# Decoder layer on one core: low parts of 18 weight blocks made by a ScalarE copy and an adding transfer instead of a VectorE subtraction

## The chip, the cores and the metric

The kernel runs on one core of one Trainium2 chip. The metric is the device time of one execution, in microseconds (us), as the median of several runs. The engines are PE (TensorE), with PEld for its weight loads, DVE (VectorE), ACT (ScalarE), POOL (GpSimd) and SP (SyncE, which here only starts transfers).

## The reference, cut to what matters

One layer for 256 tokens of 1024 features: a half-step SwiGLU FFN, a mixing block (attention beside a gated unit), a second half-step SwiGLU FFN, a final norm; each part has a shift, a scale and a gate that come from c. The change lies in the second FFN:

```
mod = c_act @ w_ada[l] + b_ada[l]
(sh1, sc1, gt1, sh2, sc2, gt2, sh3, sc3, gt3) = jnp.split(mod, N_MOD, axis=-1)
...
y = modulate(rmsnorm(h, norm_ffn2[l]), sh3, sc3)
h = h + 0.5 * gt3[:, None, :] * swiglu(y, w_ffn2_gu[l], w_ffn2_down[l])
return rmsnorm(h, norm_final)

def swiglu(x, w_gu, w_down):
    g, u = jnp.split(x @ w_gu, 2, axis=-1)
    return (jax.nn.silu(g) * u) @ w_down
```

All data is float32. The result has to be as exact as float32 products give it.

## The kernel before

**Products in three parts.** PE multiplies in float32r, a shorter form of float32. So each float32 operand is split exactly into a high part (its float32r rounding) and a low part (what is left), and each product is done three times: high by high, low of the activations by high of the weights, high of the activations by low of the weights (`mm3`, L383, and `out_rows`, L397).

**Blocks of weights.** `add_weight` (L201) makes one block of 128 x 1024 numbers, 512 KB, ready: a place `raw` (8 of them, `RBUFS`), a place `wh` and a place `wl` (10 of each, `WBUFS`); SP starts the load from DRAM into `raw` (L208); ACT copies `raw` to `wh`, which rounds it (L209); DVE writes `wl = raw - wh` (L210). `raw` is free again after that, `wh` and `wl` after the block's last product. A block of the second FFN's gate and up weights is named `gu2`, block b (0 to 10, 256 hidden features each) and quarter kq (0 to 3, 256 of the 1024 input features); a block of its down weights `d2`, b, k (k is 0 or 1).

**Order of the work in FFN 2.** `gate_up(b)` (L438) runs over the four quarters and in each over both tiles t of 128 tokens; a step `k_part` (L389) is 6 matmuls. After the third step the activations of the block before are transposed (`turn`, L426: PE `pa`, ACT `ah`, DVE `al`), after each tile's last quarter ACT makes silu and DVE the product with u (`act_t`, L419: `sg`, `a`). Then `down(b-2)` (L458) runs 24 matmuls. So one round takes 72 matmuls and 4 transposes and uses 6 blocks of weights. Blocks 0 and 1 run in another order at the end of a handwritten list of steps (`MIX`, L57).

**Who decides when a block is made.** The program's text is the order of each engine. After each `mm3` or matmul of `out_rows`, `tick` (L328) compares a model of DVE's time, `vec.t`, with one of PE's, `ten.t`. As long as DVE's is less than 1 us ahead, it writes the next item: a block of weights, if fewer than 10 are in use, or an item of the list `fill`. In FFN 2 `fill` still holds the gate `gt3`: 8 blocks `ada8_k` of 512 KB use the same `raw` places, and for each of them DVE adds `ada * c` to a sum `acc` (L249); then the sum is split (`ada_split`, L264: ACT `acch`, DVE `accl`) and PE spreads it over the partitions with 4 matmuls `pada` (`ada_row`, L275). `vec.t` grows by each instruction that is issued through `vec`.

POOL computes a few small things there (`rstd_of`, L349) and is idle for the rest of FFN 2. It has started three transfers of 4 KB before (L246).

Of the kernel before, what the change touches and what calls it, by code (L numbers as in the profile page):

```python
# [8 lines left out]
F32 = mybir.dt.float32  # L9
F32R = mybir.dt.float32r  # L10
AF = mybir.ActivationFunctionType
ALU = mybir.AluOpType
# [63 lines left out]
class Paced:  # L76
    """An engine, and the time in us that the instructions written for it so far will take."""

# [28 lines left out]
def tile_decoder_layer(ctx: ExitStack, tc, i, out):  # L107
    """The schedule is the order of this text: each engine runs what is written for it in order."""
    nc = tc.nc
# [13 lines left out]
    def unit(name, shape, dtype=F32):  # L123
        """2 KB per partition, of a common pool."""
        return units[0].tile(shape, dtype, tag="u", name=name)
# [21 lines left out]

# [1 line left out]
    c_one = const.tile([1, D], F32, name="c_one")  # L149
# [42 lines left out]

# [1 line left out]
    # A weight block arrives in float32 and is split exactly, w = wh + wl; a block of w_ada is  # L194
    # multiplied by c and summed. tick() starts the next ones: as many as have a place, and no more
    # than the vector engine does within LEAD us of the products written so far.
    weights, fill = [], []
    ready, unused, live = {}, set(), set()
    keep, fill_at, auto = [0], [0.0], [False]

    def add_weight(key, srcs, shape, n=1024):  # L201
        def run():
            nm = "_".join(str(x) for x in key)
            raw = wp.tile([P, 1024], F32, tag="raw", name=f"raw_{nm}", bufs=RBUFS)
            wh = wp.tile([P, 1024], F32R, tag="wh", name=f"wh_{nm}")
            wl = wp.tile([P, 1024], F32R, tag="wl", name=f"wl_{nm}")
            for view, src in srcs(raw[:, :n]):
                nc.sync.dma_start(view, src)  # L208
            nc.scalar.activation(wh[:, :n], raw[:, :n], AF.Copy)  # L209
            vec.tensor_tensor(wl[:, :n], raw[:, :n], wh[:, :n].bitcast(F32), op=ALU.subtract)  # L210
            ready[key] = (shape(wh[:, :n]), shape(wl[:, :n]))
            unused.add(key)
            live.add(key)

        weights.append((key, run))
# [21 lines left out]
    def ada_item(comp, k):  # L237
        """A gate: 128 rows of its columns, times c, added to the sum. A shift or a scale: 128 of
        its columns, which lie on the partitions, times c, summed."""
        def run():  # L240
            raw = wp.tile([P, 1024], F32, tag="raw", bufs=RBUFS, name=f"ada{comp}_{k}")
            if comp in GATES:
                if k == 0:
                    adaacc[comp] = const.tile([P, D], F32, tag="acc", name=f"acc{comp}", bufs=1)
                    nc.gpsimd.memset(adaacc[comp], 0.0)
                    nc.gpsimd.dma_start(adaacc[comp][0:1, :], i["b_ada"][0:1, comp * D:(comp + 1) * D])  # L246
                acc = adaacc[comp]
                nc.sync.dma_start(raw, i["w_gate"][GATES.index(comp), tsl(k), :])
                vec.scalar_tensor_tensor(acc, raw, c_col[:, k:k + 1], acc, op0=ALU.mult, op1=ALU.add)  # L249
            else:  # L250
                nc.sync.dma_start(raw, i["w_shsc"][COMPS.index(comp), tsl(k), :])
                ada_sum(comp, k, raw)

        fill.append((("ada", comp, k), run))
# [20 lines left out]
    def ada_row(comp, mul):  # L275
        """A gate as a row on every partition."""
        def run():
            r = const.tile([P, D], F32, tag="adarow", name=f"ada_row{comp}", bufs=2)
            for n in range(2):
                ah, al = adahl[comp][n]  # L280
                p = pst(f"pada{comp}_{n}")
                ten.matmul(p, onesr, ah, start=True, stop=False)
                ten.matmul(p, onesr, al, start=False, stop=True)
                nc.scalar.activation(r[:, nsl(n)], p, AF.Copy, scale=mul)
            adarow[comp] = r
        fill.append((("adar", comp), run))
# [3 lines left out]
    def ada_col(comp, ks=slice(0, KT)):  # L290
        """A shift or a scale, its features on the partitions."""
        if comp not in adacol:
            adacol[comp] = sm.tile([P, KT], F32, tag="adacol", name=f"ada_col{comp}")
        r = adacol[comp][:, ks]
        if comp in b_sh:
            vec.tensor_tensor(r, adaacc[comp][:, ks], b_sh[comp][:, ks], op=ALU.add)
        elif ks.stop - ks.start == 1:
            vec.scalar_tensor_tensor(r, adaacc[comp][:, ks], b_sc[comp][:, ks], n_w[comp][:, ks],
                                     op0=ALU.add, op1=ALU.mult)
        else:  # L300
            vec.tensor_tensor(r, adaacc[comp][:, ks], b_sc[comp][:, ks], op=ALU.add)
            vec.tensor_tensor(r, r, n_w[comp][:, ks], op=ALU.mult)
# [10 lines left out]
    def upto(items, key):  # L313
        """Runs the items up to and including the one of this name."""
        while any(k == key for k, _ in items):
            items.pop(0)[1]()

    def done(key):
        """The block of this name was used for the last time: its place goes to a later one."""
        live.discard(key)  # L320
# [26 lines left out]

# [1 line left out]
    def rstd_of(parts, name):  # L349
        """(sum of the partial mean squares + eps) ** -0.5, per token."""  # L350
        v = sm.tile([P, 1], F32, tag="var", name=f"v_{name}")
# [8 lines left out]
    def mean_sq(x, n, name, junk=None):  # L360
        """sum(x^2) / n over 512 features; n is 512 or 1024."""
        ss = sm.tile([P, 1], F32, tag="ss", name=f"ss_{name}", bufs=6)
# [4 lines left out]

# [1 line left out]
    yh = const.tile([P, KT, S], F32R, name="yh")  # L369
# [19 lines left out]
    def k_part(ps, t, kq, key, first=None, last=None):  # L389
        """A quarter of the reduction over the model's features."""  # L390
        wh, wl = need(key + (kq,))
# [5 lines left out]
    def out_rows(po, t, lh, ll, w, first, last):  # L397
        """The products that add 128 rows to po[t]; lh and ll are the operands."""
        wh, wl = w
# [11 lines left out]

# [1 line left out]
    class Ffn:  # L413
# [51 lines left out]
    class Chain:  # L465
        """After the last product of a token tile: h += gt * po, the norm, and what comes of it."""

# [33 lines left out]

# [1 line left out]
    gu1, d1, w_in, w_out = i["gu1"], i["w_ffn1_down"][0], i["w_in"], i["w_out"][0]  # L503
# [59 lines left out]

    # ---- FFN 1, its first products in slices of the reduction as the modulation arrives: the
    # steps, and OPEN, their order ----
    f1 = Ffn("1")
# [3 lines left out]
    def once(key, *before):  # L570
        """Notes a step, and that these came before it."""
        assert key not in seen and all(x in seen for x in before), key
        seen.add(key)
# [22 lines left out]
    def open_t(j, e):  # L596
        """Two slices of the features of x, turned."""
        assert (0, j) in xn and (1, j) in xn
# [66 lines left out]
    def open_m(j, x, c, t):  # L665
        """Slice j of the products of a block."""
        wh, wl = splits[j, x]
# [25 lines left out]
    def open_p():  # L693
        """Keeps the clock of the tensor engine up until there are products."""
        if "idle" not in first:
            first["idle"] = pst("idle")
        ten.transpose(first["idle"][:, 0:P], ident, ident)
# [7 lines left out]
    for b in range(NFIRST, NB):  # L705
        f1.gate_up(b, [waiting.pop(0) for _ in range(min(4, len(waiting)))])
        waiting.append(b)
        for x in DOWNS.get(b, ()):
# [3 lines left out]
            f1.down(x)  # L712
# [1 line left out]

# [38 lines left out]

# [1 line left out]
    def half_row(name):  # L755
# [31 lines left out]
    def step_gv(t):  # L787
        """gelu and layer norm of the gating unit's v."""
        once(("gv", t))
# [25 lines left out]

    # q and k: rotary embedding, then heads on the partitions
    qkT = {}
# [41 lines left out]
    def step_ga(q):  # L859
        """Four heads, both chunks."""  # L860
        once(("ga", q), ("gn", 0), ("gn", 1))
# [22 lines left out]

    # scores and softmax, queries on the partitions
    probs, sums = {}, {}
# [162 lines left out]
def _lay_out(a):  # L1049
    import numpy as np  # L1050

    def gate_up(w):
        """[block, quarter, partition, (slice, gate or up, column)]"""
        return w.reshape(4, 2, P, 2, NB, 256).transpose(4, 0, 2, 1, 3, 5).reshape(NB, 4, P, 1024)
# [45 lines left out]
```

## Time and profile before

| What | us |
|---|---|
| Median of three runs | 511.62 |
| The three runs | 511.62, 513.96, 511.62 |
| Span of the profiled execution, first to last instruction | 509.2 |
| Fastest run less that span (what lies around it) | 2.4 |

| Engine | busy us | share of the span |
|---|---|---|
| PE | 496.5 | 98% |
| DVE | 375.1 | 74% |
| ACT | 264.1 | 52% |
| POOL | 24.3 | 5% |

The page lists no time of the profiled execution other than its span, so 2.4 us are taken as lying around it, and its own time as 511.6 us, which is the median. FFN 2 runs from about 312 us to 497 us of the span. All times in the rows are counted from the span's start. Line numbers are those of the kernel before; in the changed kernel the same lines come 4 to 8 lines later.

### The profile page before, as it was taken

How to read it: one execution, taken by the hardware profiler on the slowest of the kernel's cores; microseconds unless marked ns; L12 is line 12 of the kernel's file. 1: busy time of each engine (PE TensorE's matmuls, PEld its weight loads, DVE VectorE, ACT ScalarE, POOL GpSimd, SP SyncE). 2: the span in 40 equal slices, each digit the busy share in tenths (PEclk: the TensorE clock that was granted, in tenths of full speed). 3: DMA queues.
4: the chain of work that ended last, by engine and by line, in shares of the span. 5: the costliest groups of instructions: out<-in, count | busy, mean ns of one | idle time of the engine just before them, and what ended most of it. 6: DMA issues, size and time to landing. Idle time of an engine off the chain costs nothing.

```text
span 509.2 us, 6450 instructions
## 1 busy us (share of the span) xinstructions
PE 496.5 (98%) x2297; PEld 404.7 (79%) x2297; DVE 375.1 (74%) x512; ACT 264.1 (52%) x405; POOL 24.3 (5%) x38
## 2 busy tenths in 40 slices
PE   6999999999999999999999999999999999999994
PEld 4788888888888887887788988888888888888883
DVE  4999889998787557899888999879654545455244
ACT  4655576544544443776676447864544354444112
POOL 3100000000000200100003221000000000000000
PEclk9999999999999999999999999999999999999998
DMA  8999879999998966459776768699865555540002
GB/s 281 398 371 376 328 236 340 413 408 325 338 308 314 362 208 207 136 196 322 259 258 242 240 196 287 215 325 331 340 205 189 187 168 202 181 152 1 0 2 82
DMA packets 38018, 126.38 MB, mean 248 GB/s; under 512 B 4449, under 2 KB 4449, under 8 KB 37986
## 3 DMA queue, kind: packets, MB, share of 16 engines
q1 hardware_dynamic: 37602, 125.44, 70.4%
q10 hardware_dynamic: 288, 0.52, 0.3%
q8 instruction: 18, 0.29, 0.2%
q14 instruction: 14, 0.11, 0.1%
q0 software_dynamic: 96, 0.01, 0.0%
HBM read 124.91 MB, written 1.05 MB: 247 GB/s over the span
## 4 chain that ended last, share of the span: by engine, by line
PE 92%; DVE 2%; issue 2%; DMA 1%; ACT 1%; POOL 1%; SPq 0%; POOLq 0%; ACTq 0%
PE pg L85 39%; PE po L85 21%; PE f L85 8%; PE pw L85 4%; PE pp_gv L85 2%; PE pp_v L85 2%; PE pp_q L85 2%; PE pp_k L85 2%; PE pp_gu L85 2%; PE pa L85 2%; PE psc L85 2%; DMA h<-in_x_dram 1%; PE pv L85 1%; PE pada L85 1%; PE ppT L85 1%
## 5 line engine op out<-in xcount | busy, mean ns | idle before, releaser
L85 PE MATMUL pg<-wh_gu,yh 128*128 128x512 f32 x288 | 115.4, 401 | 0.0
L85 DVE TENSOR_TENSOR wl_gu<-raw_gu,wh_gu 128x1024 fp32r<-128x1024 f32 x72 | 86.8, 1222 | 38.1 <-ACT wh_gu L209 37.9
L85 PE MATMUL pg<-wl_gu,yh 128*128 128x512 f32 x288 | 113.7, 395 | 0.0
L85 PE MATMUL pg<-wh_gu,yl 128*128 128x512 f32 x288 | 113.6, 394 | 0.0
L209 ACT ACTIVATE wh_gu<-raw_gu 128x1024 fp32r<-128x1024 f32 x72 | 74.4, 1055 | 49.3 <-PE po L85 30.6
L85 DVE TENSOR_TENSOR wl_d<-raw_d,wh_d 128x1024 fp32r<-128x1024 f32 x44 | 53.8, 1227 | 28.2 <-ACT wh_d L209 28.1
L85 PE MATMUL po<-wh_d,ah 128*128 128x512 f32 x176 | 69.1, 393 | 0.0
L85 PE MATMUL po<-wh_d,al 128*128 128x512 f32 x176 | 69.0, 392 | 0.0
L85 PE MATMUL po<-wl_d,ah 128*128 128x512 f32 x176 | 69.0, 392 | 0.0
L209 ACT ACTIVATE wh_d<-raw_d 128x1024 fp32r<-128x1024 f32 x44 | 46.4, 1059 | 35.0 <-PE pg L85 25.1
L85 PEld LDWEIGHTS pg<-wl_gu,yh 128*128 128x128 f32 x288 | 54.2, 188 | 12.7
L85 PEld LDWEIGHTS pg<-wh_gu,yl 128*128 128x128 f32 x288 | 54.3, 189 | 11.8
L85 PEld LDWEIGHTS pg<-wh_gu,yh 128*128 128x128 f32 x288 | 54.3, 189 | 11.8
L85 PEld LDWEIGHTS po<-wh_d,ah 128*128 128x128 f32 x176 | 33.1, 188 | 7.2
L85 PEld LDWEIGHTS po<-wl_d,ah 128*128 128x128 f32 x176 | 33.1, 188 | 7.1
L85 PEld LDWEIGHTS po<-wh_d,al 128*128 128x128 f32 x176 | 33.1, 188 | 7.1
L85 DVE SCALAR_TENSOR_TENSOR ada<-ada,c_row 128x1024 f32<-128x1024 f32 x32 | 38.5, 1218 | 0.0
L85 DVE SCALAR_TENSOR_TENSOR acc<-ada,cols,acc 128x1024 f32<-128x1024 f32 x24 | 30.7, 1278 | 0.1
L422 ACT ACTIVATE sg<-pg 128x256 f32<-128x256 f32 x36 | 13.7, 385 | 31.6 <-PE pg L85 31.6
L434 ACT ACTIVATE ah<-pa 128x512 fp32r<-128x512 f32 x22 | 13.2, 598 | 26.1 <-PE pa L85 26.1
L85 PE MATMUL f<-wl_first,yh 128*128 128x512 f32 x64 | 25.4, 396 | 0.9 <-DVE wl_first L85 0.9
L85 PE MATMUL f<-wh_first,yh 128*128 128x512 f32 x64 | 25.6, 400 | 0.0
(203 smaller groups left out, 712.6 us busy)
## 6 DMA issues: line engine op xcount, KB each, us to landing
raw_gu<-in_gu_dram SPq DMA_DIRECT2D x72, 512.0 KB, 4.8
raw_d<-in_w_ffn_down_dram SPq DMA_DIRECT2D x44, 512.0 KB, 5.2
ada<-in_w_shsc_dram SPq DMA_DIRECT2D x32, 512.0 KB, 5.0
ada<-in_w_gate_dram SPq DMA_DIRECT2D x24, 512.0 KB, 5.0
raw_ada<-in_w_shsc_dram SPq DMA_DIRECT2D x16, 512.0 KB, 6.8
raw_first<-in_gu_dram SPq DMA_DIRECT2D x16, 512.0 KB, 6.7
raw_wo<-in_w_out_dram SPq DMA_DIRECT2D x8, 512.0 KB, 4.4
raw_inq<-in_w_in_dram SPq DMA_DIRECT2D x4, 512.0 KB, 6.8
```

The lines of the kernel that those rows point to most:

```text
L85: return getattr(self.engine, name)(out, *args, **kw)
L209: nc.scalar.activation(wh[:, :n], raw[:, :n], AF.Copy)
L422: nc.scalar.activation(sg, ps[:, 0:256], AF.Silu)
L434: nc.scalar.activation(ah, pv, AF.Copy)
```

## The change

For the gate and up blocks of FFN 2 with b of 2 to 10 and quarter 1 or 3 (18 of its 44 gate and up blocks), ACT writes a second copy, `wl = -wh`, and POOL starts a transfer within the on-chip memory that adds `raw` to `wl`. DVE's subtraction is gone for them. All other blocks are made as before.

```diff
+    def by_dma(key):
+
+        return key[0] == "gu2" and key[1] >= 2 and key[2] % 2 == 1
...
             nc.scalar.activation(wh[:, :n], raw[:, :n], AF.Copy)
-            vec.tensor_tensor(wl[:, :n], raw[:, :n], wh[:, :n].bitcast(F32), op=ALU.subtract)
+            if by_dma(key):
+                nc.scalar.activation(wl[:, :n], wh[:, :n].bitcast(F32), AF.Copy, scale=-1.0)
+                nc.gpsimd.dma_start(wl[:, :n].bitcast(F32), raw[:, :n], accum_op=ALU.add)
+            else:
+                vec.tensor_tensor(wl[:, :n], raw[:, :n], wh[:, :n].bitcast(F32), op=ALU.subtract)
```

The rest of the diff removes comments.

The new instructions don't go through `vec`, so `vec.t` doesn't grow for them, and `tick` writes the items that follow somewhat earlier.

**ACT, from the last activations of block 1 to the transposed ones of block 0.** `wh_gu_3_1` is the copy of block 3, quarter 1, `wl_gu_3_1` its negated copy, `wh_d_1_0` that of down block 1, 0; the last number of a name is a buffer's. Before:

```order
L422 ACTIVATE sg_3194<-pg_3141 128x256
L209 ACTIVATE wh_gu_3_1_3199<-raw_gu_3_1_3198 128x1024
L209 ACTIVATE wh_gu_3_2_3205<-raw_gu_3_2_3204 128x1024
L209 ACTIVATE wh_gu_3_3_3211<-raw_gu_3_3_3210 128x1024
L434 ACTIVATE ah_3244<-pa_3239 128x512
L434 ACTIVATE ah_3259<-pa_3254 128x512
L209 ACTIVATE wh_d_1_0_3267<-raw_d_1_0_3266 128x1024
```

Now:

```order
L430 ACTIVATE sg_3196<-pg_3143 128x256
L213 ACTIVATE wh_gu_3_1_3201<-raw_gu_3_1_3200 128x1024
L215 ACTIVATE wl_gu_3_1_3202<-wh_gu_3_1_3201 128x1024
L213 ACTIVATE wh_gu_3_2_3208<-raw_gu_3_2_3207 128x1024
L213 ACTIVATE wh_gu_3_3_3214<-raw_gu_3_3_3213 128x1024
L215 ACTIVATE wl_gu_3_3_3215<-wh_gu_3_3_3214 128x1024
L213 ACTIVATE wh_d_1_0_3241<-raw_d_1_0_3240 128x1024
L442 ACTIVATE ah_3254<-pa_3249 128x512
L442 ACTIVATE ah_3272<-pa_3267 128x512
```

Two copies are added, and the copy of a down block now stands ahead of the two `ah`.

**DVE, from there to the gate's sum.** Before:

```order
L85 SCALAR_TENSOR_TENSOR acc_3007<-ada_6_3379,cols,acc_3007 128x1024
L85 TENSOR_TENSOR wl_d_2_0_3390<-raw_d_2_0_3388,wh_d_2_0_3389 128x1024
L85 TENSOR_TENSOR al_3403<-pa_3397,ah_3402 128x512
L85 SCALAR_TENSOR_TENSOR acc_3007<-ada_7_3412,cols,acc_3007 128x1024
L85 TENSOR_TENSOR wl_d_2_1_3420<-raw_d_2_1_3418,wh_d_2_1_3419 128x1024
L85 TENSOR_TENSOR accl_0_3437<-acc_3007,acch_0_3436 128x512
L85 TENSOR_TENSOR accl_1_3441<-acc_3007,acch_1_3440 128x512
```

Now:

```order
L85 SCALAR_TENSOR_TENSOR acc_3007<-ada_6_3364,cols,acc_3007 128x1024
L85 SCALAR_TENSOR_TENSOR acc_3007<-ada_7_3391,cols,acc_3007 128x1024
L85 TENSOR_TENSOR wl_d_2_0_3399<-raw_d_2_0_3397,wh_d_2_0_3398 128x1024
L85 TENSOR_TENSOR al_3412<-pa_3406,ah_3411 128x512
L85 TENSOR_TENSOR accl_0_3425<-acc_3007,acch_0_3424 128x512
L85 TENSOR_TENSOR accl_1_3429<-acc_3007,acch_1_3428 128x512
```

The sum of the gate is finished earlier in DVE's order. On PE the 4 matmuls `pada` moved with it: they stood after the seventh step of `gate_up(3)` and stand after the fifth now, 12 matmuls earlier.

**SP, the loads for the gate.** What stands in brackets is waited for; `DMASW` is a transfer that POOL started, `DMAHW` one of SP, `DVE` an instruction of DVE. Before:

```order
L208 DMA raw_gu_3_3_3210<-in_gu_dram 128x1024 [waits DMAHW4_49,DVE_49]
L248 DMA ada_2_3236<-in_w_gate_dram 128x1024 [waits DMAHW5_49,DVE_49]
L208 DMA raw_d_1_0_3266<-in_w_ffn_down_dram 128x1024 [waits DMAHW6_49,DVE_49]
L248 DMA ada_3_3278<-in_w_gate_dram 128x1024 [waits DMAHW7_49,DVE_49]
...
L248 DMA ada_6_3379<-in_w_gate_dram 128x1024 [waits DMAHW7_49,DVE_49]
```

Now:

```order
L212 DMA raw_gu_3_3_3213<-in_gu_dram 128x1024 [waits DMAHW5_49,DMAHW4_49,DVE_49]
L256 DMA ada_2_3231<-in_w_gate_dram 128x1024 [waits DMASW3_49]
L212 DMA raw_d_1_0_3240<-in_w_ffn_down_dram 128x1024 [waits DMAHW7_49,DMAHW6_49,DVE_49]
L256 DMA ada_3_3264<-in_w_gate_dram 128x1024 [waits DMASW4_49]
...
L256 DMA ada_6_3364<-in_w_gate_dram 128x1024 [waits DMASW6_49]
```

The `raw` places of `ada8_2`, `ada8_3`, `ada8_5` and `ada8_6` were those of blocks that the adding transfers read: 2,1 and 2,3 and 3,1 and 3,3 (`DMASW3` to `DMASW6`). Later loads wait for the later transfers in the same way.

## Rows read from the trace of the kernel before

**Rows 1.** The page's chain that ended last, by engine, over the whole span.
```profile
PE 92%; DVE 2%; issue 2%; DMA 1%; ACT 1%; POOL 1%; SPq 0%; POOLq 0%; ACTq 0%
```

**Rows 2.** Waits of PE, whole span (releaser: us in total, times, longest).
```profile
PE pc L85 <- DMA c_one<-in_c_dram: 2.4, 1, 2.4
...
PE tr_m L85 <- DVE z_m L85: 0.3, 1, 0.3
```

**Rows 3.** Windows: us; PE, PEld, DVE, ACT, POOL busy; clock, DMA share, GB/s.
```profile
335.00:352.00 17.00, 17.00 (x79) 13.89 (x78) 15.21 (x16) 10.15 (x13) 0.00 (x0) 1.00 0.89 314
352.00:369.00 17.00, 17.00 (x78) 13.84 (x77) 12.24 (x15) 9.53 (x13) 0.00 (x0) 1.00 0.91 351
...
437.00:454.00 17.00, 17.00 (x77) 13.88 (x76) 8.79 (x9) 7.51 (x10) 0.00 (x0) 1.00 0.57 185
```

**Rows 4.** The chain that ended last, in FFN 2: start us, us, what.
```profile
319.62 19.52 PE pg L85 x84
339.14 0.44 PE pa L85 x4
...
346.99 5.50 PE po L85 x24
352.50 4.18 PE pg L85 x18
...
362.69 0.93 PE pada L85 x4
```

**Rows 5.** The page's costliest groups: count, busy us, mean ns, idle before and releaser.
```profile
L85 DVE TENSOR_TENSOR wl_gu<-raw_gu,wh_gu 128x1024 fp32r<-128x1024 f32 x72 | 86.8, 1222 | 38.1 <-ACT wh_gu L209 37.9
...
L209 ACT ACTIVATE wh_gu<-raw_gu 128x1024 fp32r<-128x1024 f32 x72 | 74.4, 1055 | 49.3 <-PE po L85 30.6
```

**Rows 6.** Timeline of ACT in a steady round: start, us, instruction, [idle before, releaser].
```profile
399.54 1.05 ACT L209 ACTIVATE wh_gu<-raw_gu 128x1024 fp32r<-128x1024 f32 x1
402.00 1.06 ACT L209 ACTIVATE wh_gu<-raw_gu 128x1024 fp32r<-128x1024 f32 x1 [1.41 <-PE po L85]
404.76 1.06 ACT L209 ACTIVATE wh_gu<-raw_gu 128x1024 fp32r<-128x1024 f32 x1 [1.69 <-PE po L85]
407.32 1.06 ACT L209 ACTIVATE wh_d<-raw_d 128x1024 fp32r<-128x1024 f32 x1 [1.50 <-PE pg L85]
```

**Rows 7.** Timeline of ACT around the first blocks that change.
```profile
325.08 2.95 ACT L209 ACTIVATE wh_gu<-raw_gu 128x1024 fp32r<-128x1024 f32 x3
...
330.81 0.39 ACT L422 ACTIVATE sg<-pg 128x256 f32<-128x256 f32 x1 [1.84 <-PE pg L85]
...
335.27 2.94 ACT L209 ACTIVATE wh_gu<-raw_gu 128x1024 fp32r<-128x1024 f32 x3
```

**Rows 8.** Timeline of SP: the load of ada8_2.
```profile
328.80 0.33 SPq L248 DMA_DIRECT2D ada<-in_w_gate_dram  x1
```

**Rows 9.** Timeline of DVE at the end of the gate's sum.
```profile
357.78 0.69 DVE L85 TENSOR_TENSOR al<-pa,ah 128x512 fp32r<-128x512 f32 x1 [0.38 <-ACT ah L434]
358.39 1.28 DVE L85 SCALAR_TENSOR_TENSOR acc<-ada,cols,acc 128x1024 f32<-128x1024 f32 x1
...
360.72 1.29 DVE L85 TENSOR_TENSOR accl<-acc,acch 128x512 fp32r<-128x512 f32 x2
```

**Rows 10.** Loads of gate and up blocks: 72, from issue to landing.
```profile
L208 SPq DMA_DIRECT2D raw_gu<-in_gu_dram x72: 327/328/393, 47.5 to 436.1; - x72
...
DMA to landing us min/median/max: 3.1/4.8/7.6
```

**Rows 11.** Loads of ada8 blocks between 318 and 365 us, from issue to landing.
```profile
L248 SPq DMA_DIRECT2D ada<-in_w_gate_dram x6: 328/328/328, 328.8 to 347.7; - x6
...
DMA to landing us min/median/max: 4.2/5.2/5.9
```

**Rows 12.** The three 4 KB transfers that POOL started, from issue to landing.
```profile
L246 POOL DMA_DIRECT2D acc<-in_b_ada_dram x3: 511/586/862, 13.6 to 306.0; - x3
...
DMA to landing us min/median/max: 3.3/4.9/5.4
```

## The prediction

> **What bounds the kernel now.** I read the chain that ended last first: 92% of the span is PE [rows 1]. Then I asked what PE ever waits for: four waits in the whole span, 5.2 us together, the longest 2.4 us at the very start and the last one before the mixing block's products; the two ends of that list stand in [rows 2]. In FFN 2 there is none. The windows say the same: in every stretch from 335 to 454 us PE is busy for all 17.00 of 17.00 us at a granted clock of 1.00, the 2.4 GHz level [rows 3]. So the stage is bound by PE's own pace: 19.52 us / 84 = 0.232 us a matmul [rows 4], and 72 matmuls with 4 transposes make a round of 17.1 us. DVE is busy for 15.21 us of the 17.00 from 335 us on, where the gate's sum is still made, but only for 8.79 in a steady round; ACT for 10.15 and 7.51 [rows 3]. The low parts that DVE makes are taken off an engine that nobody waits for.
>
> **DVE's subtractions: removed, worth nothing.** 18 instructions of 1.222 us [rows 5] are 22.0 us of DVE's time. PE waits for none of them, so the gain on the path is 0. The bound on the gain side: if DVE's reading slowed PE's stream, the gate and up steps could at best reach the pace of the down steps, 5.50 / 24 = 0.229 us [rows 4]; 3 ns for each of the 9 x 48 = 432 matmuls of blocks 2 to 10 is 1.3 us. I take 0, since DVE works beside the down steps too.
>
> **ACT's second copies: hidden.** 18 copies of some 1.055 us, priced by the first copy of the same size [rows 5], are 19.0 us. Two fall into each round. In a steady round quarter 1's first copy ends at 400.59 and the next one begins at 402.00; quarter 3's ends at 405.82 and the next begins at 407.32 [rows 6]. Gaps of 1.4 and 1.5 us hold a copy each, so nothing behind it on ACT is later: neither the silu nor `ah`. The two in block 2 fall into a denser stretch: three copies from 325.08, then one of a down block, then 1.84 us of idling before the silu at 330.81 [rows 7]. Two more copies at the pace there (2.95 / 3 = 0.98 us) take 1.97 us, which makes that silu 0.1 us late; PE needs the place that it frees four steps of 1.4 us later. Cost 0. If ACT had no such gaps, the cost would be the copies' whole 19 us.
>
> **The waits on PE: hidden if the transfers are in time.** PE gets 18 waits for the transfers, one at the first use of each low part. A wait that is already met costs nothing visible: the down steps' first matmul waits for `ah` and follows at PE's usual pace in [rows 4]. So all depends on X, the time from POOL's issue to the landing of an adding transfer. No row shows one.
>
> **What X may be.** From below: a load of the same 512 KB took 3.1 us at least [rows 10]. From above: the slowest of POOL's transfers, 5.4 us for 4 KB [rows 12], and twice the slowest load, 7.6 us, since two operands have to be read [rows 10]: 20.6 us. I take 4.9 us, POOL's median for a transfer with almost no bytes, and twice 1.6 us, the time that the 16 engines are taken by one load (0.57 x 17.0 / 6, [rows 3]): X = 8.1 us. It is nearest the row with the same issuer; the bytes come on top.
>
> The Trainium skill ("DMA: Bandwidth & Descriptors", Anatomy of one DMA) fits a transfer started by GpSimd as about 2.0 us and its bytes at 436 GB/s. That would be 2.0 us for the 4 KB here, where the trace shows 3.3 to 5.4, so the measurement decides; by the page X would be 3.2 us, the sum would stay and the first rival below would all but go.
>
> **How much X the schedule bears.** Three places, the tightest counts.
> - The first use. Block 2, quarter 1 is copied as the first of three at 325.08 [rows 7]; its negated copy ends at 327.0. PE uses the low part in the third step of `gate_up(2)`, which ends where `pa` begins, 339.14 [rows 4]; six matmuls of 0.232 earlier plus two gives 338.2. So X may be 11.1 us. Quarter 3 is copied two copies and its own negation later, 330, and used 6 us later: more room.
> - The gate's loads. SP started `ada8_2` at 328.80 [rows 8]. Now it waits for the first transfer, until 327.0 + X = 335.1, and SP's queue behind it waits too: down block 1,0, `ada8_3` and so on. The last of these, `ada8_6`, waits for the transfer of block 3, quarter 3. On ACT five copies stand where three began at 335.27 [rows 7], so POOL starts that one at 340.2, and `ada8_6` lands at 340.2 + X + 5.2 [rows 11]. Behind it DVE has two sums of 1.28, a low part of 1.22, `al` of 0.69 and both `accl`, 1.29 [rows 5, 9]: done at 351.2 + X. PE reaches `pada` 12 matmuls earlier than before, at 362.69 - 2.79 = 359.90 [rows 4], and its fourth matmul 0.7 us later. So X may be 9.4 us. With X = 8.1 the margin is 1.3 us. `al` of block 0 and the product `a` of block 2, which are queued behind `ada8_2` and `ada8_3`, are needed by PE at 346.99 and 352.50 [rows 4]; summed the same way they bear about 11 us.
> - The steady rounds. A place `wh` comes back ten blocks later, so a block is copied 9 blocks of 2.85 us (17.1 / 6) ahead of its use; two copies off that leave 23 us for X. A load that waits for a transfer to leave its `raw` place comes 8 or 9 blocks ahead of its own copy: 23 us less the copies and 4.8 for the load leave 16 us.
>
> All transfers together: a round leaves 0.43 x 17.1 = 7.4 us of the 16 engines' time free [rows 3], and two transfers at twice a load's 1.6 us take 6.4. POOL has nothing else to do until 496 us.
>
> **Sum.** 0 for DVE, 0 for ACT, 0 for the waits: the span stays at 509.2 us, with 2.4 us around it **511.6 us**, which is also the median of the runs before.
>
> **The rivals.**
> - **Slower: the gate's chain waits for the transfers.** The place is `pada` in `gate_up(3)` and the loads behind transfers 1 to 4. Above X = 9.4 us each further microsecond is one of PE's; the first use joins in at 11.1. At 15 us it is 5.6 us: 517.2; at the upper bound of 20.6 us it is 11.2 us: 522.8. For it: the DMA engines are at 0.89 and 0.91 there [rows 3], so loads and transfers slow each other, and a load of 7.6 us in place of 5.2 would lower the limit to 7.0, which X = 8.1 passes by 1.1 us. Against it: a stall under 2.5 us still reads as no change. The Trainium skill ("SBUF — State Buffer", Who interferes with whom) says that a VectorE instruction with both inputs in SBUF contends with GpSimd's reads, and that a transfer started by GpSimd can be held up while it can't write its descriptors; no run here shows it, and one instruction of DVE more would bring X to 9.3 us. Chance 0.17.
> - **Slower: the DMA engines become the bound.** That needs more than 3.7 us of all engines for one transfer (7.4 / 2), over twice a load's 1.6. At four times, 6.4 us, a round of loads and transfers is 9.7 + 12.8 = 22.5 us, 5.4 longer than PE's; over the 8 rounds of blocks 3 to 10 that is 43 us, less the lead of 23: 531. For it: nothing but that the row is missing. Chance 0.06.
> - **Faster: DVE's or ACT's rest slows PE after all.** Then up to 1.3 us are gained, 510.3 us; more only if a stall hides in PE's busy time that the rows don't show. Chance 0.04.
> - **The change doesn't thin out DVE's order**: no, 18 subtractions are gone from it, and the sums moved up; that part is certain.
>
> **How the numbers follow.** 0.5%, 2.6 us, is about what a measurement of this kernel can tell from no change. The forecast, a stall of 0 to 2.5 us, has 0.73. Of the faster case 0.01 lies within 0.5% and 0.03 beyond. So same 0.74, slower 0.17 + 0.06 = 0.23, faster 0.03. The range reaches down to the faster case's 510.2 and up to X of nearly 16 us, 518.0; it leaves out the second rival and the upper part of the first, some 0.13.
>
> **What would show it.** Right: 54 instead of 72 of DVE's gate and up subtractions, 18 more copies on ACT, no wait of PE between 318 and 488 us, transfers that land in under 9.4 us, the chain's round still 17.1 us. Rival one: a wait of PE at `pada`, `al` or a low part between 335 and 365 us and none later, with `ada8_6` landing late. Rival two: waits of PE on low parts in every round, and a DMA share near 1 until the end. The prediction is wrong if transfers take 12 us or more, or if PE's pace of 0.232 us changes.

## The result and the profile after

The changed kernel takes 520.07 us (median of 4 runs, 517.49 to 521.51), the kernel before 511.62 beside it: a ratio of 1.0146, 95% interval 1.011 to 1.0182. It is slower by 7.5 us by that ratio, 8.5 by the medians; the prediction was no change, 511.6 us, with a range up to 518.0. The profiled execution is the longest of the four, 521.51 us with a span of 519.8 us, 10.6 more than before.

The waits of PE in the whole span answer to [rows 2]. FFN 2 had none; now it has these three (where: in us in total, times, longest):

```profile
PE pada L85 <- ACT acch L278: 4.2, 1, 4.2
...
PE pg L85 <- DVE a L85: 1.7, 1, 1.7
...
PE pada L85 <- DVE accl L85: 0.7, 1, 0.7
```

6.6 us together. 4.9 of them are at the place that the first rival named, `pada` in `gate_up(3)`; 1.7 are at the product `a` of block 2 ahead of it, for which the prediction had worked out a margin of about 11 us of X. PE waits for no low part.

The windows with the columns of [rows 3]; the third, 369 to 386 us, is new:

```profile
335.00:352.00 17.00, 17.00 (x79) 13.88 (x79) 9.48 (x10) 8.32 (x10) 1.74 (x2) 1.00 1.02 287
352.00:369.00 17.00, 10.39 (x42) 7.53 (x41) 9.90 (x11) 9.56 (x13) 1.74 (x2) 0.92 1.03 323
369.00:386.00 17.00, 17.00 (x69) 13.69 (x69) 5.75 (x6) 10.56 (x13) 1.74 (x2) 0.88 1.02 349
437.00:454.00 17.00, 17.00 (x77) 13.89 (x76) 6.25 (x8) 9.65 (x11) 1.75 (x2) 1.00 0.87 232
```

Three things are to be seen. The DMA engines went from 0.89 and 0.91 to 1.02 and 1.03: in the early stretch they are full (a share a little over 1.00 can only be an inexact reading and is read as full here). The granted clock is below 1.00 where PE has stalled and behind it. And the steady round (437 to 454) is as before for PE, with DVE down from 8.79 to 6.25 us and ACT up from 7.51 to 9.65.

The chain that ended last, in the early stretch of FFN 2 (start us, us, what), where [rows 4] had PE alone:

```profile
320.12 15.35 PE pg L85 x66
...
340.15 11.75 DMA raw_gu<-in_gu_dram
...
354.32 0.42 DVE a L85 x2
354.74 9.69 DMA raw_d<-in_w_ffn_down_dram
...
364.53 1.06 ACT wh_d L213
...
367.36 0.69 DVE accl L85
...
368.10 1.65 PE pada L85 x3
369.75 5.68 PE pg L85 x18
375.43 5.50 PE po L85 x24
```

Two loads carry it: that of block 4, quarter 0 (11.75 us), on whose copies DVE's `a` waits, and that of the down block 2,0, called `d2_2_0` below (9.69 us). ACT takes them in the order of the text, so `ah` and `acch` stand behind a copy that waits for its load:

```profile
364.53 1.06 ACT L213 ACTIVATE wh_d<-raw_d 128x1024 fp32r<-128x1024 f32 x1 [2.36 <-DMA raw_d<-in_w_ffn_down_dram]
365.50 0.58 ACT L442 ACTIVATE ah<-pa 128x512 fp32r<-128x512 f32 x1
365.97 1.14 ACT L278 ACTIVATE acch<-acc 128x512 fp32r<-128x512 f32 x2
```

The gate's sum itself was complete at 362.8 us, before the copy of `d2_2_0` could begin. This is its last instruction:

```profile
361.49 1.28 DVE L85 SCALAR_TENSOR_TENSOR acc<-ada,cols,acc 128x1024 f32<-128x1024 f32 x1 [1.21 <-DMA ada<-in_w_gate_dram]
```

From the stretch of products that answers to the first of [rows 4] to the down products behind `gate_up(3)` it is 55.31 us (320.12 to 375.43). Before, these down products began at 365.01, this row of its chain:

```profile
365.01 5.50 PE po L85 x24
```

That was 45.39 us behind 319.62 [rows 4]. So 9.9 of the 10.6 us arise here: 6.6 as waits, and some 2.5 because PE runs slowly behind them (18 products in 5.68 us against 4.18 in [rows 4]; three `pada` in 1.65 us against four in 0.93). The remaining 0.8 us are not attributed. Why PE is slow there is seen in windows of 2 us; the last three columns are clock, DMA share, GB/s:

```profile
366.00:368.00 2.00, 0.80 (x1) 0.29 (x1) 2.00 (x4) 1.11 (x3) 0.00 (x0) 0.53 1.08 340
368.00:370.00 2.00, 1.90 (x5) 1.51 (x6) 0.65 (x2) 0.81 (x2) 0.00 (x0) 0.50 1.06 272
370.00:372.00 2.00, 2.00 (x6) 1.61 (x5) 0.64 (x1) 1.41 (x3) 0.00 (x0) 0.50 1.00 369
372.00:374.00 2.00, 2.00 (x8) 1.54 (x8) 1.58 (x2) 0.97 (x1) 0.00 (x0) 0.77 1.02 420
```

0.50 is the 1.2 GHz level; it follows the idle of 4.2 us. The Trainium skill ("TensorE: Matmul & The Clock Gate", Part 1) says that an idle array falls back to 1.2 GHz; the trace agrees.

In the steady rounds ACT's gaps hold the second copy, as [rows 6] let expect, and the page's group of DVE's subtractions is down to 54 of 72:

```profile
409.95 1.05 ACT L213 ACTIVATE wh_gu<-raw_gu 128x1024 fp32r<-128x1024 f32 x1
411.04 1.06 ACT L215 ACTIVATE wl_gu<-wh_gu 128x1024 fp32r<-128x1024 f32 x1
412.42 1.06 ACT L213 ACTIVATE wh_gu<-raw_gu 128x1024 fp32r<-128x1024 f32 x1 [0.32 <-PE po L85]
```

```profile
L85 DVE TENSOR_TENSOR wl_gu<-raw_gu,wh_gu 128x1024 fp32r<-128x1024 f32 x54 | 65.1, 1223 | 42.1 <-ACT wh_gu L213 41.9
```

Over the whole of FFN 2 the transfers came about as forecast: X had been put at 8.1 us, and it is

```profile
L216 POOL DMA_DIRECT2D wl_gu<-raw_gu x18: 862/872/953, 328.0 to 468.9; - x18
...
DMA to landing us min/median/max: 4.7/6.5/12.2
```

But the two transfers of block 3, issued at 338.2 and 341.2 us, are the slowest of the 18. On the second of them the prediction's sum for the gate rests. The same view for these two alone:

```profile
L216 POOL DMA_DIRECT2D wl_gu<-raw_gu x2: 862/872/881, 338.2 to 341.2; - x2
...
DMA to landing us min/median/max: 11.8/12.0/12.2
```

The page's part on DMA queues gives what they took of the engines (packets, MB, share of 16 engines' span):

```profile
q1 hardware_dynamic: 37602, 125.44, 67.7%
q0 software_dynamic: 2688, 9.45, 10.1%
```

10.1% of 519.8 us over 18 transfers is 2.9 us of all 16 engines for one, twice the 1.47 us of a 512 KB load (67.7% of 519.8 us for 125.44 MB). That too is near the 3.2 assumed. What is far off, beside these two, is the loads' time, median from issue to landing between 335 and 370 us, first before, then after:

```profile
raw_gu<-in_gu_dram SPq DMA_DIRECT2D x11, 512.0 KB, 5.8
...
raw_d<-in_w_ffn_down_dram SPq DMA_DIRECT2D x4, 512.0 KB, 7.3
```

```profile
raw_gu<-in_gu_dram SPq DMA_DIRECT2D x8, 512.0 KB, 12.8
raw_d<-in_w_ffn_down_dram SPq DMA_DIRECT2D x6, 512.0 KB, 10.4
```

And SP, which had no such transfers to wait for before, now waits for the places that transfers still read (318 to 372 us):

```profile
SPq L256 <- DMA wl_gu<-raw_gu: 16.4, 4, 8.3
SPq L212 <- DMA wl_gu<-raw_gu: 8.6, 2, 4.6
```

### The profile page after: what moved, and what is told of

Same layout as the page of the kernel before. It is cut to its first block, busy times and chain, and to the rows that moved or that the text cites. A ratio compares the mean times of both kernels' runs of the same rounds, so it can differ in the third digit from the quotient of the medians.

```text
span 519.8 us, 6482 instructions
## 1 busy us (share of the span) xinstructions
PE 500.3 (96%) x2297; PEld 406.5 (78%) x2297; DVE 354.4 (68%) x494; ACT 283.0 (54%) x423; POOL 40.2 (8%) x56
## 3 DMA queue, kind: packets, MB, share of 16 engines
q1 hardware_dynamic: 37602, 125.44, 67.7%
q0 software_dynamic: 2688, 9.45, 10.1%
## 4 chain that ended last, share of the span: by engine, by line
PE 86%; DMA 5%; DVE 3%; issue 2%; ACT 2%; POOL 1%; SPq 0%; POOLq 0%; ACTq 0%
PE pg L85 35%; PE po L85 20%; PE f L85 8%; PE pw L85 4%; DMA raw_gu<-in_gu_dram 2%; PE pp_gv L85 2%; PE pp_v L85 2%; PE pp_gu L85 2%; PE pp_k L85 2%; PE pp_q L85 2%; DMA raw_d<-in_w_ffn_down_dram 2%; PE psc L85 2%; PE pa L85 2%; DMA h<-in_x_dram 1%; PE pv L85 1%
## 5 line engine op out<-in xcount | busy, mean ns | idle before, releaser
L85 DVE TENSOR_TENSOR wl_gu<-raw_gu,wh_gu 128x1024 fp32r<-128x1024 f32 x54 | 65.1, 1223 | 42.1 <-ACT wh_gu L213 41.9
L85 PEld LDWEIGHTS pg<-wh_gu,yh 128*128 128x128 f32 x288 | 54.7, 190 | 14.1 <-DVE a L85 2.1
L213 ACT ACTIVATE wh_d<-raw_d 128x1024 fp32r<-128x1024 f32 x44 | 46.4, 1058 | 30.3 <-PE pg L85 16.1
L216 POOL DMA_DIRECT2D wl_gu<-raw_gu x18 | 15.8, 877 | 136.7 <-PE po L85 69.8
```

What stands on the lines that cost most here:

```text
L85: return getattr(self.engine, name)(out, *args, **kw)
L216: nc.gpsimd.dma_start(wl[:, :n].bitcast(F32), raw[:, :n], accum_op=ALU.add)
```

## The experiments

**Theory.** In the early stretch the 16 DMA engines are nearly full with loads. The transfers (a) take engine time there, so loads take longer, and (b) hold `raw` places, so loads start later. Either makes `d2_2_0` late, ACT waits for it ahead of `acch`, and PE at `pada`. **Rivals:** the new order of the text alone; ACT's second copies; a cost of every transfer wherever it stands.

Each run is told with its median, and the ratio to the kernel before on the same chip with its 95% interval.

**1. The order alone, and the order with the copies.** In place of the copy and the transfer, DVE makes the low part, not counted by the planner:

```diff
-                nc.scalar.activation(wl[:, :n], wh[:, :n].bitcast(F32), AF.Copy, scale=-1.0)
-                nc.gpsimd.dma_start(wl[:, :n].bitcast(F32), raw[:, :n], accum_op=ALU.add)
+                nc.vector.tensor_tensor(wl[:, :n], raw[:, :n], wh[:, :n].bitcast(F32), op=ALU.subtract)
```

> The changed kernel's order on PE and SP, but VectorE makes all low parts by a difference again, and there are no negated copies and no transfers (VectorE has 18 instructions more than the planner counted). Theory (the transfers take time of the 16 DMA engines where the gate's and the weights' loads already take 0.9 of it): 511 to 513 us, no wait of PE above 1 us between 335 and 370 us, DMA share back to about 0.9 there, loads to 3 to 8 us. Rival order (the products of the gate come 12 matmuls earlier and the loads in another order, and that alone costs the time): 517 to 521 us.

511.82 us, 0.9997 (0.9977 to 1.0017). No wait of PE in FFN 2; share 0.94 and 0.95. Keeping ACT's copy and letting DVE add `raw` to it:

```diff
-                nc.gpsimd.dma_start(wl[:, :n].bitcast(F32), raw[:, :n], accum_op=ALU.add)
+                nc.vector.tensor_tensor(wl[:, :n], raw[:, :n], wl[:, :n].bitcast(F32), op=ALU.add)
```

> The changed kernel with its order and its 18 negated copies on ScalarE, but the addition is made by VectorE; no transfers. Theory (DMA engines' time): 511 to 513 us, DMA share about 0.9 between 335 and 370 us. Rival copies (ScalarE's second copies push the down block's copy and the sum's copies behind them): PE waits for ah, acch or a low part as in the changed kernel, 515 to 520 us.

511.84 us, 1.0008 (0.9989 to 1.0027), no wait. So neither the order nor the 18 copies cost anything that these intervals of 0.2 to 0.3% to either side could tell; it is the transfers. That run had a share of 1.00 at 363 GB/s:

```profile
352.00:369.00 17.00, 17.00 (x77) 13.55 (x76) 12.88 (x15) 10.99 (x15) 0.00 (x0) 1.00 1.00 363
```

A full share by itself thus stalls nobody; it matters what comes late.

**2. Where the transfers stand.** The condition `key[1] >= 2` becomes `>= 5`, `>= 4`, and `in (2, 3)`:

```diff
-        return key[0] == "gu2" and key[1] >= 2 and key[2] % 2 == 1
+        return key[0] == "gu2" and key[1] >= 5 and key[2] % 2 == 1
```

> As the changed kernel, but transfers only from block 5 on: 12 of the 18, all after the gate's sum is made. Theory: no wait of PE in FFN 2, 511 to 512.5 us. Rival steady cost (each transfer costs some time wherever it stands, two thirds of the 8.5 us here): 516 to 518 us.

511.86 us, 0.9999 (0.9984 to 1.0014), no wait of PE in FFN 2.

> As the changed kernel, but transfers only from block 4 on: 14 of the 18. The first two are issued at about 352 to 360 us, behind the start of the load of d2_2_0, on which the gate's products hang. Theory: the gate's products wait for less than 1 us: 511 to 513 us. If any transfer in the dense stretch costs: 514 to 518 us.

513.18 us, 0.2 above the range of the theory, on a chip where the kernel before takes 512.67: 1.0007 (0.9993 to 1.0021), no wait. The first two transfers start at 350.5 and 355.9 us, still in the dense stretch (share 1.03 from 352 to 369 us), but the load of `d2_2_0` had been issued at 347.4.

> As the changed kernel, but only the four transfers of blocks 2 and 3, the ones made while the gate's columns are loaded. Theory (the loss lies wholly in the early stretch): 516 to 521 us, with the wait at the gate's products. If the loss comes from all 18: 513 to 514 us.

517.56 us, 1.0108 (1.0083 to 1.0134). PE waits 2.5 us for `a` and 0.4 for `accl`, and the clock falls to 0.50. The time is in the range of the theory, the place is not: the longer wait is at `a`, behind the load of block 4, quarter 0 (12.7 us), and hardly at the gate's products. So 14 transfers from block 4 on are free, and the 4 of blocks 2 and 3 alone cost 1.1%. Whether the other 14 add something where the loads are late already can't be told by the times: the interval overlaps with that of the changed kernel, 1.011 to 1.0182. The profiled executions hint that it does: with all 18 PE waits 6.6 us instead of 2.9, and `d2_2_0`, beside which the transfers of block 4 then run, took 9.7 us instead of 7.7.

**3. The order of before, with all transfers.**

```diff
+                vec.t += 0.06 + n / 960
                 nc.scalar.activation(wl[:, :n], wh[:, :n].bitcast(F32), AF.Copy, scale=-1.0)
```

> The changed kernel with all its copies and transfers, but the planner counts the subtractions that were removed, so that PE and SP keep the order of before, in which the gate's products come 12 matmuls (2.8 us) later. Theory: the loads are as slow as in the changed kernel, and PE waits for about 2.8 us less at the gate's products and as long for the product of block 2: 514 to 518 us. Rival order: 511.6 us, no wait.

522.27 us, 1.0204 (1.0175 to 1.0234): both expectations were wrong, the theory about the size. The gate's products come later, but in this order the copy of the next down block, too, stands ahead of `acch` on ACT, and its load is late as well:

```profile
367.22 1.06 ACT L213 ACTIVATE wh_d<-raw_d 128x1024 fp32r<-128x1024 f32 x1 [4.50 <-DMA raw_d<-in_w_ffn_down_dram]
368.18 1.14 ACT L279 ACTIVATE acch<-acc 128x512 fp32r<-128x512 f32 x2
```

**4. Places or engines.** First the places: DVE makes all low parts, and two tiny transfers, one behind the other, keep each `raw` place taken.

```diff
+                hold = sm.tile([P, 4], F32, tag="hold", name=f"hold_{nm}", bufs=1)
+                nc.gpsimd.dma_start(hold, wh[:, 0:4].bitcast(F32))
+                nc.gpsimd.dma_start(hold, raw[:, 0:4])
```

> The changed kernel's order on PE and SP; VectorE makes all low parts, no negated copies. Behind each of the 18 differences POOL issues two transfers of 16 bytes per partition, one after the other, the second from the raw place: the place is held some 6 to 11 us longer, as by an adding transfer, and the 16 DMA engines get next to no work. Theory places (the held raw places stop SP's queue, the loads start late; in the changed kernel the load of d2_2_0 was issued 5.8 us later than with the order alone): SP waits for these transfers by 10 us and more in 318 to 400 us, PE waits at the gate's products, 514 to 519 us. Theory engines (the transfers' 2.9 us of all 16 engines make every load slow): loads of 5 to 8 us, no wait of PE above 1 us, 511 to 513 us.

521.25 us, 1.02 (1.0171 to 1.023), more than the 514 to 519 us of the theory. The engines are less busy than before the change (share 0.71 and 0.82), yet PE waits 2.9 and 0.9 us at `pada`. SP's waits, 318 to 372 us:

```profile
SPq L258 <- DMA hold_gu<-raw_gu: 20.3, 4, 5.9
...
SPq L212 <- DMA hold_gu<-raw_gu: 5.9, 1, 5.9
```

Then the engines: DVE makes all low parts, and each adding transfer goes from `wh` into a tile that nobody reads (`c_row`, no longer needed, and a new one).

```diff
+                nc.gpsimd.dma_start(sink, wh[:, :n].bitcast(F32), accum_op=ALU.add)
```

> The changed kernel's order on PE and SP; VectorE makes all low parts, no negated copies. At each of the 18 places POOL issues an adding transfer of the same size from the high part into a tile that nobody reads: the same work for the 16 DMA engines, but no raw place is held and nobody waits for it (two units fewer in the pool of small tiles are paid for by this: 21 of 22). Theory engines: loads of 8 to 14 us in 335 to 370 us, PE waits at the gate's products, 514 to 520 us. Theory places: no wait of PE above 1 us, 511 to 513 us. If both this and the run before stay under 513 us, it takes both together.

520.36 us, 1.0187 (1.0148 to 1.0227), just above the 514 to 520 us of the theory. SP waits for no transfer, but the loads are slow from 335 to 370 us, and PE waits 4.0 and 0.7 us at `pada`:

```profile
raw_gu<-in_gu_dram SPq DMA_DIRECT2D x9, 512.0 KB, 13.4
raw_d<-in_w_ffn_down_dram SPq DMA_DIRECT2D x5, 512.0 KB, 12.4
```

Either alone suffices. How they share the work in the changed kernel is seen at the load of `d2_2_0`, in us counted from the first `pa` of FFN 2 (339.48 us in the changed kernel; 340.94, 339.87 and 341.09 in the others):

| Kernel | issued | took | landed |
|---|---|---|---|
| Order alone | 8.0 | 6.2 | 14.1 |
| Changed | 15.3 | 9.7 | 25.0 |
| Places held only | 17.4 | 4.3 | 21.7 |
| Engines only | 10.5 | 12.8 | 23.4 |

With the order alone ACT copies it at 16.1 with data that landed at 14.1. The changed kernel's load lands 10.8 us later than that: 7.3 by its late issue, 3.5 by its own time. The held run holds the places somewhat longer than the real transfers do, since its issue comes 2.2 us later still; it shows that the mechanism suffices, not its exact share.

**5. The price of adding.** The transfers overwrite:

```diff
-                nc.gpsimd.dma_start(wl[:, :n].bitcast(F32), raw[:, :n], accum_op=ALU.add)
+                nc.gpsimd.dma_start(wl[:, :n].bitcast(F32), raw[:, :n])
```

> The changed kernel whole, but its 18 transfers overwrite instead of adding (left out: the addition, so that these low parts hold the whole weight). Theory: an adding transfer takes the 16 engines 2.9 us because it reads two operands and writes one; a plain one takes about a load's 1.5 us and lands some 2 us earlier, so both the engines and the raw places are relieved: the loss is 2 to 7 us, 514 to 519 us. If the adding costs nothing: 519 to 521 us, as the changed kernel.

517.76 us, 1.0099 (1.0082 to 1.0115): the loss is 5.1 us by the medians instead of 8.5, within what was expected. The interval just touches that of the changed kernel (1.011 to 1.0182), so the gain is likely but not clear of noise. The traces are clear: X falls, and so does the engines' time, 4.6% of 516.7 us, 1.3 us for one:

```profile
DMA to landing us min/median/max: 2.9/4.1/8.9
```

```profile
q0 software_dynamic: 2688, 9.45, 4.6%
```

So adding doubles what a transfer takes of the engines (2.9 against 1.3 us). The Trainium skill ("DMA: Bandwidth & Descriptors", Anatomy of one DMA) would make it an estimated 3.2 us from issue to landing by its fit; that is near the 2.9 of the fastest plain one here, and no adding one in any run took under 4.6.

**6. What PE loses at the gate's products.** They are put behind `gate_up(9)` (their result is needed only at the end):

```diff
-        fill.append((("adar", comp), run))
+        if comp == 8:
+            late.append(run)
+        else:
+            fill.append((("adar", comp), run))
...
         f2.gate_up(b, waiting)
+        if b == 9:
+            late.pop()()
```

> The changed kernel whole, but the four products of the gate come behind gate_up(9) and no longer in gate_up(3); their result is used only at the end. Theory (the stall is that of an in-order engine at these products; the late loads hurt nobody else but the product of block 2): the waits for acch and accl go, with them the lower clock behind them; the wait of 1.7 us at pg stays: 512.5 to 515 us. If the late loads delay everything in FFN 2, the wait only moves to the next step: 517 us or more.

516.28 us, 1.0095 (1.0068 to 1.0121): the loss is 4.5 us by the medians instead of 8.5. That is outside both expectations, a little above the 512.5 to 515 us of the theory and below the 517 of the other; and the interval overlaps with that of the changed kernel, so the gain is likely but not clear of noise. The waits at `pada` and the low clock are gone; but the next `a` now waits as well, which the stall had covered:

```profile
PE pg L85 <- DVE a L85: 3.1, 2, 2.0
```

In the next run the gate's products stay in `gate_up(3)`, and the wait ahead of them is filled with idle products:

```diff
+                if comp == 8 and n == 0:
+                    for x in range(18):
+                        nc.tensor.matmul(p, onesr, yh[:, 0:2, :], start=True, stop=True)
```

> The changed kernel whole, with 18 matmuls of 128x512 more ahead of the gate's products, which overwrite the same place in PSUM and fill the 4.2 us in which PE waits there (their result is not used). Theory (the clock at 1.2 GHz behind the idle costs about 2.3 us of its own): the wait for acch falls under 0.7 us, granted clock 1.00 behind it, 516.5 to 519 us. Without such a cost: 519 to 521 us, as the changed kernel.

520.77 us, 1.0183 (1.0155 to 1.0212): a miss, in the range that was expected without a cost of the clock. The clock itself does what was expected, as the same 2 us show, but the median gains nothing:

```profile
368.00:370.00 2.00, 2.00 (x10) 1.62 (x9) 0.00 (x0) 1.18 (x3) 0.00 (x0) 1.00 1.02 262
```

In its profiled execution `acch` was done at 365.9 us and the idle products went on until 368.3. The filler has a fixed length, while the stall varies from run to run (the changed kernel's spans go from 515.8 to 519.8 us). In the two profiled executions the stretch that took 55.31 us above took 51.83 here (321.60 to 373.43); but `acch` was also ready sooner after the transposes, so the clock's part can't be read from that. What the clock costs in the median stays open; in one profiled execution it is the 2.5 us read above.

**7. The second rival, provoked.** All four quarters from block 5 on:

```diff
-        return key[0] == "gu2" and key[1] >= 2 and key[2] % 2 == 1
+        return key[0] == "gu2" and key[1] >= 5
```

> Transfers only from block 5 on, but for all four quarters: 24 of them, four in a round. Four at 2.9 us and six loads at 1.47 us ask 20.5 us of the 16 engines in a round of 17.1. Theory: the DMA engines become the bound there, DMA share 0.98 and more between 380 and 460 us, and once the lead of some 20 us is used up, PE waits for weights in the last rounds: 513 to 525 us. If the engine time of a transfer is less than thought (share under 0.95): 511 to 512.5 us, no wait.

512.82 us, 0.9994 (0.9979 to 1.001): the share came as expected, the waits of PE did not.

```profile
380.00:460.00 80.00, 80.00 (x356) 65.16 (x355) 17.02 (x23) 55.49 (x62) 16.30 (x19) 1.00 1.05 291
```

From 375 to 450 us, 17 transfers and 25 loads share them so:

```profile
q0 software_dynamic: 2431, 8.84, 59.8%
q1 hardware_dynamic: 3430, 12.51, 44.3%
```

That is 2.6 us for a transfer and 1.3 for a load (59.8% and 44.3% of 75 us), so four and six of them ask 18.5 us in a round of 17.1: a deficit of 1.4 us and not of 3.4 (the two shares add up to more than 1, so these figures are rough). SP waits for transfers 18 times there (65.7 us together), and PE never. Over the six rounds of blocks 5 to 10 the deficit adds up to some 8 us, less than the lead of 16 to 23 us that the prediction worked out for the steady rounds; that the lead takes it up is argued from these numbers and wasn't tried. In a steady round of this run DVE is busy for 4 us of 17 and PE is no faster.

No version beats the kernel before. PE has no wait in FFN 2 there, and three versions that take DVE's work off without a stall (transfers from block 5, from block 4, all quarters from block 5) measure 0.9999, 1.0007 and 0.9994.

## Why the prediction was wrong

- **PE bounds FFN 2, and DVE's 18 subtractions are worth nothing: right.** With the transfers harmless, DVE's saving gave no time at all (experiments 2 and 7). Its upper bound of 1.3 us did not show either.
- **ACT's second copies are hidden: right.** The order with copies and without transfers is at 1.0008.
- **X = 8.1 us: near the median, wrong where it was used.** The median of the 18 is 6.5 us, and 2.9 us of the engines against 3.2 assumed. The nearness is partly luck: the fastest transfer, 4.7 us with 2.9 of them for the engines, leaves an estimated 1.8 us for the rest, where the sum had put 4.9. And X was used for the transfers of block 3, in the dense stretch, which took 11.8 and 12.2 us. The prediction named 12 us or more as a sign that it is wrong.
- **"So X may be 9.4 us. With X = 8.1 the margin is 1.3 us": this step failed, twice.** First, it priced the transfer of block 3, quarter 3 by itself at 8.1 us, though loads fill the engines beside it. It took 12.2 us, 2.8 over the limit that the step itself had worked out. The load of `ada8_6` behind it was priced well (4.5 us measured, 5.2 assumed) and landed at 357.9 us, where the sum has 353.5. Second, it followed only the gate's loads. The load that came last was another one, `d2_2_0`, which stands behind the gate's loads in SP's queue and whose copy stands ahead of `ah` and `acch` on ACT. Against the order alone it was issued 7.3 us later and took 9.7 us instead of 6.2; the median load of a gate and up block took 12.8 us there, instead of 5.8 before the change. The gate's sum was complete at 362.8 us; PE reached `pada` at 362.4 and went on at 366.6. So the gate's own loads account for an estimated 1 us of the wait of 4.2, and the copy of `d2_2_0` ahead of `acch` for the rest; no run separates them.
- **`a` of block 2 "bears about 11 us": wrong as well.** The sum followed `ada8_2` and `ada8_3`; `a` came late behind the load of block 4, quarter 0 (11.75 us), whose low part DVE makes ahead of it.
- **"A round leaves 0.43 x 17.1 = 7.4 us of the 16 engines' time free": right for the steady round, and summed only there.** The same sum for 335 to 369 us, from numbers that were in the text, would have told: shares of 0.89 and 0.91 [rows 3] leave 0.10 x 34 = 3.4 us, and the four transfers that POOL starts there ask 4 x 3.2 = 12.8 by the assumed price, 11.7 by the measured one. The overflow of 8 to 9 us has to appear as lateness of loads. Such a sum doesn't tell whether PE waits: with transfers from block 4 on, two ask 5.8 us of the same 3.4, and nothing was lost.
- **The first rival came true**, for most of the wait at its place, with the mechanism that it names (loads and transfers slow each other) and with the late places beside it. Its chance of 0.17 was too low, since the sentence for it had the 0.89 and 0.91 in it and did not multiply them out. It was also priced as one wait at full clock: 6.6 us of waits became 9.9 on the path in the profiled execution, some 2.5 of them behind the stall at 1.2 GHz, which the prediction didn't price.
- **The second rival** (engines bound in every round) did not happen: a transfer takes 2.9 us, under the 3.7 where it decides, and the round is 17.1 us as before.

## What to carry to other kernels

A transfer that replaces an instruction is paid in two currencies, engine time and the time for which its source place stays taken; sum both in the densest stretch of the stage, not in its steady state, and multiply the share that is left by the stretch's length before calling a transfer hidden. Follow every load that stands behind the delayed ones in the issuing queue to the in-order engine that consumes it: the one that stalls PE may belong to another tensor than the one that was changed. Where offloading is wanted anyway, start it behind the loads for which an in-order engine will soon wait: here the same transfers from block 4 on cost nothing, although the first two still start in the dense stretch.

## What was not expected of the hardware

- Adding doubles the engines' time of a transfer within the on-chip memory (512 KB: 2.9 us of all 16 engines, 1.3 us without adding), and each alone, held places with the engines less busy than before the change (share 0.71 and 0.82) or busy engines without held places, cost about as much as both together (2.0%, 1.9% and 1.5%).
- A stall of PE can cost more than itself, though no median here shows how much: behind waits of 4.2 us (the changed kernel), 2.9 us (places held only) and 2.5 us (blocks 2 and 3) the granted clock was at 0.50 for some microseconds; behind waits of 2.0 and 2.1 us (gate late, filled wait) it stayed at 1.00. With the plain transfers, two waits of 1.9 and 1.0 us close together brought it to 0.57.
- DMA engines that are full for 80 us cost nothing in experiment 7, where the loads have a lead (that the lead is the reason is argued), and a few microseconds of overflow came with a loss of 1.5% in the early stretch.
